# Rolling a matrix along its rows: hand-made semaphores, and the last 64 columns of 128 rows as a ladder of small DMAs

## The chip, the cores and the metric

The kernel runs on one core of one Trainium2 chip. The metric is the device time of one execution in microseconds (us), lower is better. It was timed 13 times.

## What is computed

```python
def setup_inputs():
    return {
        "x": np.random.randn(8192, 8192).astype(np.float32),
        "shift": 100,
    }

def reference(x: np.ndarray, shift: int) -> np.ndarray:
    return np.roll(x, shift, axis=1)
```

Every row of 8192 float32 (32,768 B) is rotated to the right by 100 columns: `out[r, 100:] = x[r, :8092]` and `out[r, :100] = x[r, 8092:]`. Nothing is calculated; 268.4 MB are read from the chip's main memory (HBM) and 268.4 MB are written to it.

## The kernel before

With `shift` 100 the kernel has `s = 100`, `a = 128` (s rounded up to 128) and `g = a - s = 28`. It splits every output row in two.

The **bulk** is `out[:, 128:] <- x[:, 28:8092]`, 8064 columns or 32,256 B of every row, copied from HBM to HBM with no stop in on-chip memory. The row number is taken apart as `c*64 + e*4 + j` with 16 values of `e` and 4 of `j`. One DMA (L37) takes one `j`, all 16 `e` and 32 of the 128 `c`: 512 row pieces, 16.5 MB. The `e` dimension stands first, so that each of the 16 DMA engines gets the rows of one `e`, 32 row pieces of each DMA. There are 16 such DMAs, issued in turn by two queues: SP takes `j` = 0 and 2, ACT takes `j` = 1 and 3, eight DMAs each.

The **heads** are `out[:, :128]`, 512 B of every row. They take two stages (`k` = 0, 1) of 4096 rows each, by way of on-chip tiles. POOL issues three DMAs (L67) that load, for rows with `q` = 1 to 3 of each group of four, 128 contiguous values that straddle the row boundary (the last 100 of the row before and the first 28 of the row itself), and two more (L68, L71) for the parts that remain. VectorE then puts the pieces together in a tile `h` (L69, L72), and POOL stores it with four DMAs (L76) for each stage.

The kernel has no order written out by hand: the framework that builds it adds all waits. It gives each DMA one of a fixed set of semaphores, eight for the DMAs of SP and ACT together and eight for POOL's, so that the fifth DMA of SP (and of ACT) waits until its first has landed, the sixth for the second, and so on, and POOL's second L68 and L71 wait for earlier loads. At the end SP waits for the last use of every semaphore, and a barrier of all engines ends the program (shown at L107, the line of the `with` in the launch function; L93 is the program's construction with its first barrier).

Of the kernel before, what the change touches and what calls it, by code (L numbers as in the profile page):

```python
# [1 line left out]

# [4 lines left out]


@with_exitstack
def kernel(  # L10
    ctx: ExitStack,
    tc: tile.TileContext,
    x: bass.AP,
    shift: int,
    out: bass.AP,
):
    nc = tc.nc
    n_rows, n_cols = x.shape
    s = shift % n_cols
    a = -(-s // 128) * 128  # L20
    g = a - s
    P = nc.NUM_PARTITIONS
    engines = [nc.sync, nc.scalar]
    n_chunks = 16
    rows = n_rows // n_chunks

    xm = x.rearrange("(c e j) w -> j e c w", e=16, j=4)  # L30
    om = out.rearrange("(c e j) w -> j e c w", e=16, j=4)
    depth = n_rows // 64 // 4
    for c in range(4):
        for j in range(4):
            if a < n_cols:
                cs = slice(c * depth, (c + 1) * depth)
                engines[j % 2].dma_start(out=om[j, :, cs, a:], in_=xm[j, :, cs, g:n_cols - s])  # L37
    if a == 0:
        return


    if a > 512:
        for i in range(n_chunks):
            r = slice(i * rows, (i + 1) * rows)
            nc.gpsimd.dma_start(out=out[r, :s], in_=x[r, n_cols - s:])
            if g > 0:
                nc.gpsimd.dma_start(out=out[r, s:a], in_=x[r, :g])
        return

    Q, J = 4, 8
    n_st = n_rows // (P * Q * J)
    reads = ctx.enter_context(tc.tile_pool(name="reads", bufs=n_st))
    heads = ctx.enter_context(tc.tile_pool(name="heads", bufs=n_st))
    xt = x.rearrange("(k p j q) c -> k q p j c", q=Q, j=J, p=P)
    ot = out.rearrange("(k p j q) c -> k q p j c", q=Q, j=J, p=P)
    tiles = []  # L60
    for k in range(n_st):
        t = reads.tile([P, Q - 1, J, a], x.dtype)
        h = heads.tile([P, Q, J, a], x.dtype)
        for q in range(1, Q):
            lead = bass.AP(tensor=x.tensor, offset=(k * P * J * Q + q) * n_cols - s,
                           ap=[[J * Q * n_cols, P], [Q * n_cols, J], [1, a]])
            nc.gpsimd.dma_start(out=t[:, q - 1], in_=lead)  # L67
        nc.gpsimd.dma_start(out=h[:, Q - 1, :, :s], in_=xt[k, Q - 1, :, :, n_cols - s:])  # L68
        nc.vector.tensor_copy(h[:, :Q - 1, :, :s], t[:, :, :, :s])  # L69
        if g > 0:  # L70
            nc.gpsimd.dma_start(out=h[:, 0, :, s:], in_=xt[k, 0, :, :, :g])  # L71
            nc.vector.tensor_copy(h[:, 1:, :, s:], t[:, :, :, s:])  # L72
        tiles.append(h)
    for k, h in enumerate(tiles):
        for q in range(Q):
            nc.gpsimd.dma_start(out=ot[k, q, :, :, :a], in_=h[:, q])  # L76


# [1 line left out]
_INS = ['x', 'shift']  # L80
_OUTS = [((8192, 8192), 'float32')]

_NUMBERS = {'shift': 100}


# [26 lines left out]
```

## Time and profile before

| What | Value |
|---|---|
| Time, median of 13 runs | 820.45 us (816.65 to 823.09) |
| The profiled execution's own time | 820.08 us |
| Its span, first to last instruction | 818.3 us |
| VectorE busy | 3.7 us |
| POOL busy | 16.1 us |
| DMA packets and bytes | 10784, 272.63 MB |
| Bulk DMAs | 8 on SP and 8 on ACT, 16128 KB each |
| Head DMAs on POOL | 10 loads, 8 stores |

How to read it: SP, ACT and POOL only hand out transfers; the 16 DMA engines carry them out, each taking row pieces (packets) from three queues, which the profile names q1, q10 (the two hardware queues, of SP and of ACT) and q0 (POOL's). "GB/s" counts the bytes that DMAs moved; a byte copied from HBM to HBM counts once there, but is a read and a write for the HBM. "DMA share" is the mean busy share of the 16 engines. The span leaves out what lies around it, here 820.08 - 818.3 = 1.78 us.

### The profile page before, as it was taken

How to read it: one execution, taken by the hardware profiler on the slowest of the kernel's cores; microseconds unless marked ns; L12 is line 12 of the kernel's file. 1: busy time of each engine (PE TensorE's matmuls, PEld its weight loads, DVE VectorE, ACT ScalarE, POOL GpSimd, SP SyncE). 2: the span in 40 equal slices, each digit the busy share in tenths (PEclk: the TensorE clock that was granted, in tenths of full speed). 3: DMA queues.
4: the chain of work that ended last, by engine and by line, in shares of the span. 5: the costliest groups of instructions: out<-in, count | busy, mean ns of one | idle time of the engine just before them, and what ended most of it. 6: DMA issues, size and time to landing. Idle time of an engine off the chain costs nothing. (4 is left out here: it accounts for less than half of the span.)

```text
span 818.3 us, 93 instructions
## 1 busy us (share of the span) xinstructions
DVE 3.7 (0%) x4; POOL 16.1 (2%) x22
## 2 busy tenths in 40 slices
DVE  0000000000000000000000000000000000000000
POOL 3000001000010000000000000000000000000000
DMA  9999999999999999999999999999999999999996
GB/s 309 334 333 336 335 343 329 342 334 337 347 337 344 342 347 339 342 347 337 340 340 346 341 328 330 326 333 337 328 333 330 328 328 337 326 326 334 331 331 262
DMA packets 10784, 272.63 MB, mean 333 GB/s; under 512 B 544, under 2 KB 544, under 8 KB 2592
## 3 DMA queue, kind: packets, MB, share of 16 engines
q10 hardware_dynamic: 4224, 132.12, 46.8%
q1 hardware_dynamic: 4224, 132.12, 46.8%
q0 software_dynamic: 2336, 8.39, 4.7%
HBM read 268.44 MB, written 268.44 MB: 656 GB/s over the span
## 5 line engine op out<-in xcount | busy, mean ns | idle before, releaser
L76 POOL DMA_DIRECT2D out_dram<-h x8 | 6.9, 957 | 170.8 <-DMA h<-in_x_dram 144.7
L67 POOL DMA_DIRECT2D t<-in_x_dram x6 | 5.4, 911 | 0.8 <-PEq L107 0.8
L69 DVE COPY h<-t 128x2400 f32<-128x2400 f32 x2 | 2.8, 1410 | 208.4 <-DMA t<-in_x_dram 208.4
L71 POOL DMA_DIRECT2D h<-in_x_dram x2 | 1.8, 882 | 28.7 <-DMA t<-in_x_dram 28.7
L68 POOL DMA_DIRECT2D h<-in_x_dram x2 | 1.8, 884 | 26.8 <-DMA t<-in_x_dram 26.8
L72 DVE COPY h<-t 128x672 f32<-128x672 f32 x2 | 1.0, 504 | 0.0
L93 POOL MEMSET const-float32-0.0<- 128x1 f32 x1 | 0.1, 98 | 0.2 <-issue 0.2
L93 POOL MEMSET const-bfloat16-1.0<- 128x1 bf16 x1 | 0.1, 101 | 0.0
L93 POOL MEMSET const-float32-1.0<- 128x1 f32 x1 | 0.1, 98 | 0.0
L93 POOL MEMSET const-uint8-127<- 128x1 uint8 x1 | 0.1, 98 | 0.0
## 6 DMA issues: line engine op xcount, KB each, us to landing
out_dram<-in_x_dram ACTq DMA_DIRECT2D x8, 16128.0 KB, 401.6
out_dram<-in_x_dram SPq DMA_DIRECT2D x8, 16128.0 KB, 402.4
out_dram<-h POOLq DMA_DIRECT2D x8, 512.0 KB, 183.9
t<-in_x_dram POOLq DMA_DIRECT2D x6, 512.0 KB, 118.3
h<-in_x_dram POOLq DMA_DIRECT2D x2, 400.0 KB, 151.8
h<-in_x_dram POOLq DMA_DIRECT2D x2, 112.0 KB, 146.4
```

Source lines behind the costliest of these rows:

```text
L67: nc.gpsimd.dma_start(out=t[:, q - 1], in_=lead)
L68: nc.gpsimd.dma_start(out=h[:, Q - 1, :, :s], in_=xt[k, Q - 1, :, :, n_cols - s:])
L69: nc.vector.tensor_copy(h[:, :Q - 1, :, :s], t[:, :, :, :s])
L71: nc.gpsimd.dma_start(out=h[:, 0, :, s:], in_=xt[k, 0, :, :, :g])
L72: nc.vector.tensor_copy(h[:, 1:, :, s:], t[:, :, :, s:])
L76: nc.gpsimd.dma_start(out=ot[k, q, :, :, :a], in_=h[:, q])
L93: nc = _bacc.Bacc("TRN2", target_bir_lowering=False, num_devices=1)
```

## The change

- All DMAs, waits and copies stand in one critical section (`tc.tile_critical()`), in which the framework adds no waits of its own. The kernel has its own semaphores: `bulk0` and `bulk1` for the bulk of SP and ACT, `rest`, `landed0/1` for the loads of the two head stages, `paired` for the copies of VectorE and `stored` for the stores of the heads. SP, ACT and POOL each wait at their end for all that they issued.
- The bulk is cut into `c` = 0-32, 32-64, 64-96, 96-126 and 126-128; the last cut, the rows from 8064 on, ends at column `v` = 8128 (8000 columns wide). Each queue so issues ten bulk DMAs.
- The last 64 columns of the last 128 rows are copied by 30 small DMAs. SP, after its bulk, issues 15: 8 rows of 64 columns, then 15, 14, ... 2 rows with 47, 46, ... 34 columns. ACT issues the remaining columns of these rows (15 rows of 17, 14 of 18, ... 2 of 30) and a last one with the 64 columns of the very last row. In the program's order ACT's 15 stand ahead of ACT's bulk, as they are issued in the loop's pass for SP.
- The heads keep their DMAs and copies, in the same order.

The diff, without the branch for shifts that are not used here and without setup lines:

```diff
-    engines = [nc.sync, nc.scalar]
-    n_chunks = 16
-    rows = n_rows // n_chunks
+    rings = (nc.sync, nc.scalar)
 ...
-    depth = n_rows // 64 // 4
-    for c in range(4):
-        for j in range(4):
-            if a < n_cols:
-                cs = slice(c * depth, (c + 1) * depth)
-                engines[j % 2].dma_start(out=om[j, :, cs, a:], in_=xm[j, :, cs, g:n_cols - s])
+    blocks = n_rows // 64
 ...
+    with tc.tile_critical():
+        expect = {}
+
+        def issue(eng, sem, o, i):
+            eng.dma_start(out=o, in_=i).then_inc(sem, 16)
+            expect[sem] = expect.get(sem, 0) + 16
+
+        rest = nc.alloc_semaphore("rest")
+        for q, ring in enumerate(rings):
+            bulk = nc.alloc_semaphore(f"bulk{q}")
+            if a < n_cols:
+                v = n_cols - 64
+                for c0, c1, hi in ((0, 32, n_cols), (32, 64, n_cols), (64, 96, n_cols),
+                                   (96, blocks - 2, n_cols), (blocks - 2, blocks, v)):
+                    for j in range(q, 4, 2):
+                        issue(ring, bulk, om[j, :, c0:c1, a:hi], xm[j, :, c0:c1, g:hi - s])
+                if q == 0:
+                    r = n_rows - 128
+                    for k in (8, *range(15, 1, -1)):
+                        w = 64 if k == 8 and r == n_rows - 128 else 32 + k
+                        issue(ring, bulk, out[r:r + k, v:v + w], x[r:r + k, v - s:v + w - s])
+                        if w < 64:
+                            issue(nc.scalar, rest, out[r:r + k, v + w:], x[r:r + k, v + w - s:n_cols - s])
+                        r += k
+                    issue(nc.scalar, rest, out[r:, v:], x[r:, v - s:n_cols - s])
+            if bulk in expect:
+                ring.wait_ge(bulk, expect[bulk])
+        if rest in expect:
+            nc.scalar.wait_ge(rest, expect[rest])
 ...
-        for q in range(1, Q):
-            nc.gpsimd.dma_start(out=t[:, q - 1], in_=lead)
-        nc.gpsimd.dma_start(out=h[:, Q - 1, :, :s], in_=xt[k, Q - 1, :, :, n_cols - s:])
-        nc.vector.tensor_copy(h[:, :Q - 1, :, :s], t[:, :, :, :s])
+            for q in range(1, Q):
+                issue(pooled, landed, t[:, q - 1], lead)
+            issue(pooled, landed, h[:, Q - 1, :, :s], xt[k, Q - 1, :, :, n_cols - s:])
+            if g > 0:
+                issue(pooled, landed, h[:, 0, :, s:], xt[k, 0, :, :, :g])
+            nc.vector.wait_ge(landed, expect[landed])
+            nc.vector.tensor_copy(h[:, :Q - 1, :, :s], t[:, :, :, :s]).then_inc(paired, 1)
 ...
+        for k in range(n_st):
+            pooled.wait_ge(paired, (k + 1) * per)
+            for q in range(Q):
+                issue(pooled, stored, ot[k, q, :, :, :a], heads[k][:, q])
 ...
+        if stored in expect:
+            pooled.wait_ge(stored, expect[stored])
```

More of the change, by code (lines that the diff above doesn't have):

```diff
@@ L38 @@
[L38 to L45, printed above, removed]
-            if g > 0:
[L47 to L63, printed above, removed]
-        for q in range(1, Q):
-            lead = bass.AP(tensor=x.tensor, offset=(k * P * J * Q + q) * n_cols - s,
-                           ap=[[J * Q * n_cols, P], [Q * n_cols, J], [1, a]])
-            nc.gpsimd.dma_start(out=t[:, q - 1], in_=lead)
-        nc.gpsimd.dma_start(out=h[:, Q - 1, :, :s], in_=xt[k, Q - 1, :, :, n_cols - s:])
-        nc.vector.tensor_copy(h[:, :Q - 1, :, :s], t[:, :, :, :s])
[L70 to L73, printed above, removed]
@@ L74 @@
-    for k, h in enumerate(tiles):
-        for q in range(Q):
-            nc.gpsimd.dma_start(out=ot[k, q, :, :, :a], in_=h[:, q])
+    blocks = n_rows // 64
+    Q, J = 4, 8
+    narrow = 0 < a <= 512
+    n_st = n_rows // (P * Q * J) if narrow else 0
+    pool = ctx.enter_context(tc.tile_pool(name="heads", bufs=1))
+    reads = [pool.tile([P, Q - 1, J, a], x.dtype, name=f"reads{k}") for k in range(n_st)]
+    heads = [pool.tile([P, Q, J, a], x.dtype, name=f"heads{k}") for k in range(n_st)]
+    with tc.tile_critical():
[6 more added lines that the diff above has]
+            bulk = nc.alloc_semaphore(f"bulk{q}")
+            if a < n_cols:
+                v = n_cols - 64
[16 more added lines that the diff above has]
+            nc.scalar.wait_ge(rest, expect[rest])
+        pooled = nc.gpsimd
+        paired = nc.alloc_semaphore("paired")
+        stored = nc.alloc_semaphore("stored")
+        xt = x.rearrange("(k p j q) c -> k q p j c", q=Q, j=J, p=P)
+        ot = out.rearrange("(k p j q) c -> k q p j c", q=Q, j=J, p=P)
+        n_pair = 0
+        for k in range(n_st):
+            t, h = reads[k], heads[k]
+            landed = nc.alloc_semaphore(f"landed{k}")
+            for q in range(1, Q):
+                lead = bass.AP(tensor=x.tensor, offset=(k * P * J * Q + q) * n_cols - s,
+                               ap=[[J * Q * n_cols, P], [Q * n_cols, J], [1, a]])
+                issue(pooled, landed, t[:, q - 1], lead)
+            issue(pooled, landed, h[:, Q - 1, :, :s], xt[k, Q - 1, :, :, n_cols - s:])
+            if g > 0:
+                issue(pooled, landed, h[:, 0, :, s:], xt[k, 0, :, :, :g])
+            nc.vector.wait_ge(landed, expect[landed])
+            nc.vector.tensor_copy(h[:, :Q - 1, :, :s], t[:, :, :, :s]).then_inc(paired, 1)
+            n_pair += 1
+            if g > 0:
+                nc.vector.tensor_copy(h[:, 1:, :, s:], t[:, :, :, s:]).then_inc(paired, 1)
+                n_pair += 1
+        per = n_pair // n_st if n_st else 0
+        for k in range(n_st):
+            pooled.wait_ge(paired, (k + 1) * per)
+            for q in range(Q):
+                issue(pooled, stored, ot[k, q, :, :, :a], heads[k][:, q])
+        if a > 0 and not narrow:
+            for r in range(0, n_rows, 512):
+                issue(pooled, stored, out[r:r + 512, :s], x[r:r + 512, n_cols - s:])
+                if g > 0:
+                    issue(pooled, stored, out[r:r + 512, s:a], x[r:r + 512, :g])
+        if stored in expect:
+            pooled.wait_ge(stored, expect[stored])
```

## The prediction

> **What bounds the kernel now.** I read the page's strip of 40 slices and its table of queues first, then the windows over stretches of the span, then the issues of L37, then the waits of SP's queue. The page:
>
> ```profile
> DMA  9999999999999999999999999999999999999996
> GB/s 309 334 333 336 335 343 329 342 334 337 347 337 344 342 347 339 342 347 337 340 340 346 341 328 330 326 333 337 328 333 330 328 328 337 326 326 334 331 331 262
> ...
> q10 hardware_dynamic: 4224, 132.12, 46.8%
> q1 hardware_dynamic: 4224, 132.12, 46.8%
> q0 software_dynamic: 2336, 8.39, 4.7%
> HBM read 268.44 MB, written 268.44 MB: 656 GB/s over the span
> ```
>
> The 16 DMA engines are busy from the second slice to the last but one, and the three shares add up to 98.3%. There is no stretch without a transfer, so only a higher rate or a shorter start or end can save time. Which of the two limits it, engines or memory, is seen at the end, in the windows:
>
> ```profile
> core 0: us, DVE busy (x) POOL busy (x), PEclk, DMA share, GB/s
> 0.00:5.00 5.00, 0.00 (x0) 3.91 (x9) 1.00 0.63 206
> 5.00:10.00 5.00, 0.00 (x0) 3.45 (x4) 1.00 0.97 335
> ...
> 600.00:700.00 100.00, 0.00 (x0) 0.00 (x0) 1.00 1.00 331
> ...
> 790.00:800.00 10.00, 0.00 (x0) 0.00 (x0) 1.00 0.92 329
> 800.00:805.00 5.00, 0.00 (x0) 0.00 (x0) 1.00 0.81 323
> 805.00:810.00 5.00, 0.00 (x0) 0.00 (x0) 1.00 0.75 323
> 810.00:812.00 2.00, 0.00 (x0) 0.00 (x0) 1.00 0.60 258
> 812.00:814.00 2.00, 0.00 (x0) 0.00 (x0) 1.00 0.75 323
> 814.00:816.00 2.00, 0.00 (x0) 0.00 (x0) 1.00 0.38 161
> 816.00:818.30 2.30, 0.00 (x0) 0.00 (x0) 1.00 0.00 0
> ```
>
> From 790 us on some engines have nothing left, yet 92% of them move 329 GB/s and 75% (12 of 16) still 323. The bound is thus what all engines share, the HBM at about 2 x 330 = 660 GB/s, and not the engine: 323/12 = 27 GB/s is what one engine does when fewer compete, against 331/16 = 20.7 in the middle. The packet records say the same: 32,256 B take 1.19 us at the least and 1.47 at the median. The stamps of the last bulk landings show who is early: one engine is through at 758.5 us, three at 796 to 803, twelve between 813.6 and 817.4.
>
> What is lost at the ends: from 0 to 5 us (335-206)*5/335 = 1.9 us; from 810 us on (75*2 + 10*2 + 172*2 + 333*2.3)/333 = 3.8 us, of which 0.94 lies behind the last landing at 817.36. So the ends hold under 6 us together, most of it latency.
>
> ```profile
> L37 SPq DMA_DIRECT2D out_dram<-in_x_dram x4: 607/643/97766, 0.7 to 2.8; - x4
> L37 ACTq DMA_DIRECT2D out_dram<-in_x_dram x4: 670/927/99802, 0.7 to 3.4; - x4
> ...
> SPq L37 <- DMA out_dram<-in_x_dram: 47.8, 4, 17.0
> ```
>
> These are the L37 issues that fall in the first 100 us, and SP's own waits. Three issues of each queue take 0.6 to 0.95 us, the fourth 98 us: it is held until the queue has room, so nearly three DMAs always stand ready (each lasts about 103 us). The waits for semaphores, 47.8 us in four, are spent with such a queue full.
>
> **What the Trainium skill says.** "DMA: Bandwidth & Descriptors", section "Queues, rings and completion order": an engine goes round the queues that have work, packet by packet, and all queues share the same 16 engines. The equal 46.8% agree. The same page, "Why a DMA increments its semaphore by 16 and not by 1": a DMA from SP or ACT uses as many engines (at most 16) as divide its outer dimension, from the lowest number up. So the ladder lies on engines 0 and 1 most and hardly on 14; no transfer of before shows this. The same page, "Specifications": below 512 B a transfer is a read-modify-write. All ladder rows are 256 B or less. The pieces of 400 and 112 B here go to on-chip memory, so no row of this trace prices one from HBM to HBM. "HBM Reference", "Specifications (TRN2)": 716 GB/s for the stack that two cores share; the measured 656 is 92% of it.
>
> **The change part by part.** Against the profiled execution, span 818.3.
>
> 1. *Waits between bulk DMAs go* (SP's 47.8 us and ACT's like them). Worth 0: the queues hold work for 200 to 300 us meanwhile, and even the engine that runs ahead by 59 us (758.5 against 817.4) leaves them non-empty. Were the cover gone, it would be up to 17 us for each. POOL's waits between loads (26.8 and 28.7 us) go too; its loads stay in the same order in one queue that is served packet by packet. The heads end by 466 us, 350 before the end, so 0.
> 2. *Gate at the entry.* Entering the section adds a no-op on SP for which all others wait. The barriers of before need 0.04 to 0.12 us from signal to wake-up; I take +0.15 (0.05 to 0.4) on the first transfer. It can't be negative, as the first barrier stays.
> 3. *ACT's 15 small DMAs stand ahead of its bulk.* Issues at 0.67 to 0.95 us: 15 * 0.67 = 10 us (up to 14) for which ACT's first bulk DMA is late. SP's queue alone must feed the engines meanwhile. It can: the trace's first 32 packets all come from SP's queue, and the second of each engine took 1.31 to 1.35 us, shorter than the 1.47 median. So 0 (at most 5 us, half of 10, were one queue to run at half rate, which those packets exclude). Of this remains a shift: SP gets ahead by 10/1.4 = 7 packets for each engine, and at the end ACT runs alone for about as many.
> 4. *Bulk recut.* Per queue and engine 32*8 = 256 row pieces as before, two DMAs more, so two completion writes of 9 ns. The 64 columns taken out are 128*256 B / 16 = 2 KB for each engine, 0.08 us at 27 GB/s: -0.1 together.
> 5. *SP's ladder behind its bulk.* 15 issues, but they enter the queue as soon as there is room, at some 500 to 600 us (before, the eighth issue ended at 498.7), so the issue is hidden under 200 us of bulk. What counts is the engine's time. Engines 0 and 1 get 15 pieces, and so down to 2 on engine 13 and one on 14. Lower bound of a piece: 10 ns by its bytes (256 B at 27 GB/s), as a completion write's 9 ns. Upper: POOL's loads, 4096 B read from HBM in small rows, average 0.46 us in the first 60 us, three times their 0.15 us of bytes; a read that waits on a loaded HBM may cost as much for one row. I take 0.15 us, between: 15*0.15 = 2.2 us on engines 0 and 1. It falls after SP's last bulk packet, in the last 10 us, where 12 engines each run at their own limit and nothing hides it. Which engines are early the trace doesn't tell; if engine 0 is of the twelve late ones (3 in 4), which end within 3.8 us, it moves the end by part of its load. I take +0.9 (0 to 6, from 10 ns and 0.46 us).
> 6. *ACT's ladder at the start*: the same pieces while memory is the bound and others take what an engine leaves: 0 to +0.3, I take 0.1.
> 7. *Gate at the exit.* Each queue waits itself, SP waits for all, then the old final barrier: two more hops, +0.2 (0 to 0.5).
>
> Sum: 0.15 - 0.1 + 0.9 + 0.1 + 0.2 = +1.25, span 819.5, own time 821.3. The profiled execution lies 0.37 below the median of 820.45; against the median it is 821.7. I forecast **821.7 us**, no change by a hair: 0.2% is 1.64 us, about what a measurement of this kernel can tell. The case's own range is 819.8 to 824.
>
> **The rivals.**
>
> *Slower: the ladder stalls its engines.* At 0.46 us a piece, engines 0 and 1 get 6.9 us behind their bulk, and engines 2 to 5 nearly as much, where only 3.8 us of spread lie. +5, so about 825.5. For it: rows under 512 B, and reads that wait at a loaded HBM. Against: even the 112 B rows of POOL's loads come 27 to a packet of 3024 B in 0.49 us, 18 ns each, so small rows can be piped. It decides from about 0.25 us a piece.
>
> *Faster: the two queues out of step are kinder to the HBM.* Before, ACT's row piece is the neighbour of SP's and lands 3 us later throughout; now they are 7 packets or more apart. The rate isn't a constant of nature: slices go from 326 to 347 GB/s, and once the heads are done they stay near 330. One engine that drifted out of the herd lands two DMAs (64 row pieces) in 88.2 us from 669 to 757 us, 1.38 us a piece, where the herd needed 1.58 (101 us, from 616.7 to 717.6). If the mean rises by 0.8%, 820.45 - 6.5 = 814. Against: HBM traffic is near 660 GB/s whatever the mix (with the heads, 343 GB/s counted, of which some 19 are heads and load it once: 2*343 - 19 = 667). An end in which all engines stop together would belong here too, for at most 2 us.
>
> *The change doesn't do what it says: ACT's small DMAs are stuck behind SP's blocked fourth issue.* If the two queues share what makes the descriptors, ACT's bulk would begin after 50 us or later, and SP's be done by half time. As one queue feeds the engines, the time stays about 821. Against: ACT's fourth and fifth issues ended 2.6 and 5.0 us after SP's, not in the same breath.
>
> **How the numbers follow.** Forecast 0.52 (same 0.33, slower 0.17, faster 0.02), stalling ladder 0.19 (slower), kinder HBM 0.22 (faster 0.21, same 0.01), stuck queue 0.07 (same 0.04, slower 0.02, faster 0.01). Together faster 0.24, same 0.38, slower 0.38. The range 814 to 827 takes in most of the stalling ladder (to about +6.5) and half of the faster case; some 0.2 lie outside.
>
> **What will show it.** Right: 330 GB/s in the middle as before, SP's bulk through some 10 us ahead of ACT's, ladder packets near 0.15 us, the first bulk at 2.3 us. Step 3 is wrong if the DMA share falls in the first 15 us; step 5 if the ladder's packets take 0.4 us and the engines that end last are those that carry most of it; the rate's case holds if the slices after 450 us change by over 1%. The forecast fails if the middle's rate moves either way, which no sum of instructions can give.

## The result, and the profile after

| | Before | After |
|---|---|---|
| Median time | 820.56 us (48 runs) | 825.59 us (823.26 to 830.76, 11 runs) |
| Ratio | | 1.0067, 95% interval 1.0052 to 1.0083 |
| Span of the profiled execution | 818.3 us | 824.5 us |
| First bulk packet starts | 2.18 us | 2.49 us |
| Last packet ends | 817.03 us | 823.06 us |
| Last landing | 817.36 us | 823.39 us |
| From the last landing to the end of the span | 0.94 us | 1.06 us |

The change costs 5 us. The rows for packets and landings are from the trace's packet records and landing stamps. The page of the changed kernel:

```profile
GB/s 305 337 344 335 336 335 334 337 338 338 335 343 334 339 345 341 333 338 345 331 335 328 330 326 333 326 332 338 330 329 324 326 330 335 327 329 319 336 326 245
DMA packets 11372, 272.63 MB, mean 331 GB/s; under 512 B 1132, under 2 KB 1132, under 8 KB 3180
...
q10 hardware_dynamic: 4526, 132.12, 47.7%
q1 hardware_dynamic: 4510, 132.13, 47.2%
q0 software_dynamic: 2336, 8.39, 3.7%
HBM read 268.44 MB, written 268.44 MB: 651 GB/s over the span
```

588 packets are new, all under 512 B: the ladders' row pieces and the additional completion writes. They hold no visible share of the engines' time, but the mean rate is 651 GB/s where it was 656. Where that is lost, the windows show (GB/s is the last column), first the changed kernel, then the kernel before over the same three middle stretches:

```profile
5.00:10.00 5.00, 0.00 (x0) 5.00 (x7) 1.00 0.99 336
10.00:15.00 5.00, 0.00 (x0) 0.41 (x1) 1.00 0.91 293
15.00:20.00 5.00, 0.00 (x0) 0.00 (x0) 1.00 1.03 367
...
20.00:200.00 180.00, 1.83 (x2) 3.48 (x4) 1.00 1.00 337
200.00:500.00 300.00, 1.83 (x2) 3.47 (x4) 1.00 1.00 337
500.00:780.00 280.00, 0.00 (x0) 0.00 (x0) 1.00 1.00 329
...
805.00:810.00 5.00, 0.00 (x0) 0.00 (x0) 1.00 0.86 310
...
812.00:814.00 2.00, 0.00 (x0) 0.00 (x0) 1.00 0.74 306
...
816.00:818.00 2.00, 0.00 (x0) 0.00 (x0) 1.00 0.60 257
...
820.00:822.00 2.00, 0.00 (x0) 0.00 (x0) 1.00 0.34 144
822.00:824.50 2.50, 0.00 (x0) 0.00 (x0) 1.00 0.00 0
```

```profile
20.00:200.00 180.00, 1.83 (x2) 5.23 (x6) 1.00 1.00 336
200.00:500.00 300.00, 1.83 (x2) 3.47 (x4) 1.00 1.00 341
500.00:780.00 280.00, 0.00 (x0) 0.00 (x0) 1.00 0.99 330
```

The engines are as busy as before in the middle (share 1.00), and from 200 us on they still move less. From the packet records, with the bytes of the heads counted half as they touch the HBM once, 255.30 MB are through by 780 us instead of 256.90; 1.13 MB of these 1.60 are lost between 200 and 500 us. At 330 GB/s they are 4.8 us (the later start included) of the 6.2 by which the profiled spans differ. The other 1.2 us come in the tail: from 812 us on the engines end one by one (shares 0.74, 0.60 and 0.34: twelve, ten and five of 16), where in the kernel before twelve stopped within 3.8 us. The exit adds 0.1.

The ladder itself can be followed, as its packets have a size of their own for each DMA (an extract of the packet records; one packet per engine):

```
ACT's ladder, start of the packets, us
 68 B, 15 engines    5.6 ..  5.9
 72 B, 14 engines    8.6 ..  9.6
 76 B, 13 engines   12.2 .. 14.2
 ...
116 B,  3 engines   46.2 .. 48.5
120 B,  2 engines   50.4 .. 52.3
 16 B, 16 engines   16.4 .. 55.3   (ACT's bulk follows)
each of these takes 9 to 13 ns; SP's ladder packets take 13 to 18 ns
```

A step is 3 to 4 us although a packet takes 11 ns. Between two of them each engine moves two 32,256 B pieces of SP's queue (counted in e4 below): the small packet uses one turn of the round between queues and its completion write another. So ACT's queue gets to its bulk after 16 us on the engine with no row of the ladder (the first bulk packet starts at 19.7 us), and after 55 us on the one with the whole of it. That ACT's queue did issue in time is shown by its line for the first 14 us: 17 issues, while SP's fourth was held for 82 us.

```profile
L44 ACTq DMA_DIRECT2D out_dram<-in_x_dram x17: 571/737/1560, 0.9 to 13.8; - x17
...
L44 SPq DMA_DIRECT2D out_dram<-in_x_dram x4: 598/694/82342, 1.0 to 3.1; - x4
```

### The profile page after: what moved, and what is told of

It reads as the page before. It is cut to its first block, busy times and chain, and to the rows that moved or that the text cites. A ratio compares the mean times of both kernels' runs of the same rounds, so it can differ in the third digit from the quotient of the medians.

```text
span 824.5 us, 130 instructions
## 1 busy us (share of the span) xinstructions
DVE 3.7 (0%) x4; POOL 16.1 (2%) x22
## 5 line engine op out<-in xcount | busy, mean ns | idle before, releaser
L44 POOL DMA_DIRECT2D out_dram<-heads x8 | 7.0, 1006 | 217.5 <-DVE heads L96 217.5
L44 POOL DMA_DIRECT2D reads<-in_x_dram x6 | 5.4, 910 | 1.1 <-PEq L140 1.1
L93 DVE COPY heads<-reads 128x2400 f32<-128x2400 f32 x2 | 2.8, 1410 | 227.5 <-DMA heads<-in_x_dram 227.5
L44 POOL DMA_DIRECT2D heads<-in_x_dram x4 | 3.5, 882 | 0.0
```

What stands on the lines that cost most here:

```text
L44: eng.dma_start(out=o, in_=i).then_inc(sem, 16)
L93: nc.vector.tensor_copy(h[:, :Q - 1, :, :s], t[:, :, :, :s]).then_inc(paired, 1)
```

## The experiments

All times are against the kernel before on the same chip and in the same rounds. First, four kernels that take the change apart.

**e1: the critical section alone.**

```diff
-                                   (96, blocks - 2, n_cols), (blocks - 2, blocks, v)):
+                                   (96, blocks, n_cols)):
-                if q == 0:
-                    r = n_rows - 128
...
```

> The critical section with its own semaphores, the bulk in four cuts of full width, no recut and no ladder. Theory A (ACT's ladder ahead of its bulk spends one turn of every engine's round for each small packet and each completion write, so that ACT falls behind SP, by 30 turns on engine 0 and 2 on engine 15): this is the kernel before within 1.5 us, 820.6 plus 0.3 for the gates, about 821. Theory B (the ladders cost the engines time at the end): also 821. Theory C (the section itself, with deeper queues and no waits between bulk DMAs, lowers the rate from 200 us on): about 824 to 825, with 329 GB/s between 200 and 500 us where before has 333 or more.

Measured: 821.31 against 820.17, ratio 1.0023 (1.0013 to 1.0033). The rate in the middle stays (340 GB/s from 200 to 500 us, 332 from 500 to 780), so the section and the missing waits don't lower it. But from the last landing to the end of the span it takes 2.16 us, not 0.94. The waits of SP's queue, of e1 and then of the changed kernel:

```profile
SPq L40 <- DMA out_dram<-in_x_dram: 312.6, 1, 312.6
SPq L40 <- POOLq L40: 0.9, 1, 0.9
```

```profile
SPq L40 <- DMA out_dram<-in_x_dram: 156.1, 1, 156.1
SPq L40 <- ACTq L40: 1.9, 1, 1.9
```

At the exit of the section SP waits for the others, and POOL drains, which takes 1.1 us, only once SP's own wait is over. In e1 that stands open behind the last landing. In the changed kernel SP is through at 821.33 us and ACT at 823.41, so POOL's drain is hidden behind ACT's last packets.

**e2: with the recut, no ladder.**

```diff
-                                   (96, blocks - 2, n_cols), (blocks - 2, blocks, v)):
+                                   (96, blocks - 2, n_cols), (blocks - 2, blocks, n_cols)):
-                if q == 0:
-                    r = n_rows - 128
...
```

> As the first kernel, with the last bulk cut split into 30 and 2 blocks at full width, no ladder. Theories A and B: 821, as the first kernel. Theory C: as the first kernel, 824 to 825. Only if the split at the end matters by itself does it differ from the first kernel by over 1 us.

Measured: 822.10 against 820.17, ratio 1.0026 (1.0014 to 1.0038). No different from e1: the recut costs nothing that shows.

**e3: ACT's ladder moved behind ACT's bulk.**

```diff
-                        if w < 64:
-                            issue(nc.scalar, rest, out[r:r + k, v + w:], x[r:r + k, v + w - s:n_cols - s])
                         r += k
-                    issue(nc.scalar, rest, out[r:, v:], x[r:, v - s:n_cols - s])
+                else:
+                    r = n_rows - 128
+                    for k in (8, *range(15, 1, -1)):
+                        w = 64 if k == 8 and r == n_rows - 128 else 32 + k
+                        if w < 64:
+                            issue(ring, bulk, out[r:r + k, v + w:], x[r:r + k, v + w - s:n_cols - s])
+                        r += k
+                    issue(ring, bulk, out[r:, v:], x[r:, v - s:n_cols - s])
```

> The changed kernel with ACT's 15 small DMAs moved behind ACT's bulk; all else the same. Theory A: ACT's bulk starts at 1 us as SP's does, the loss goes, about 821. Theory B: both ladders now stand unhidden at the end, so it stays at 825.6 or gets worse, up to 828, with a DMA share that falls before the last landing. Theory C: 825.

Measured: 826.43 against 820.17, ratio 1.0076 (1.0063 to 1.0090), as theory B has it. But the engines are not what is held up. The windows of e3's end:

```profile
816.00:818.00 2.00, 0.00 (x0) 0.00 (x0) 1.00 0.41 176
818.00:820.00 2.00, 0.00 (x0) 0.00 (x0) 1.00 0.23 29
820.00:822.00 2.00, 0.00 (x0) 0.00 (x0) 1.00 0.00 0
822.00:824.00 2.00, 0.00 (x0) 0.00 (x0) 1.00 0.00 0
824.00:826.40 2.40, 0.00 (x0) 0.00 (x0) 1.00 0.00 0
```

No packet runs after 819.54 us, yet the last landing is stamped 824.28. An engine puts its share of the 30 small DMAs through in half a microsecond, and their completions arrive one after the other, 4.74 us in all (0.33 of it any last packet needs). The last stamps are evenly 0.17 to 0.18 us apart: one engine, with the completions of both queues in a single series. (The next expectations take 4.74/30 = 0.16 us, close to that as this engine carries most of the 30.) With the exit that makes 6.9 us behind the last packet where before has 1.27; the 5.6 between them are nearly all of e3's loss. Its middle is sound (331 GB/s from 500 to 780 us). So e3 removes one loss and brings another of the same size.

**e4: ACT's ladder replaced by 15 DMAs that all use 16 engines.**

```diff
-                    for k in (8, *range(15, 1, -1)):
...
+                    for n in range(15):
+                        r = n_rows - 128 + n // 2 * 16
+                        w = v + n % 2 * 32
+                        issue(nc.scalar, rest, out[r:r + 16, w:w + 32], x[r:r + 16, w - s:w + 32 - s])
+                    issue(ring, bulk, out[n_rows - 16:, v + 32:], x[n_rows - 16:, v + 32 - s:n_cols - s])
```

> ACT's ladder ahead of its bulk is replaced by 15 DMAs of 16 rows by 32 columns, so that every engine spends the same 15 small packets and 15 completion writes; SP has one such DMA at its end and no ladder. Theory A in its first form (what counts is that ACT's queue lags SP's by 30 turns, on whichever engines): 825 to 827. Theory A in its second form (what counts is that the lag differs from engine to engine, which pulls the engines apart): 821. Theory B: 821, as no ladder stands at the end. Theory C: 825.

Measured: 823.91 against 820.17, ratio 1.0043 (1.0028 to 1.0058): between the two forms of theory A, and the changed kernel's interval begins inside this one's. ACT's first bulk DMA landed at about 158 us, SP's at 60. As all engines have the same ladder here, the turns can be counted: before ACT's first bulk packet, at 53.4 us, SP's queue started 30.4 pieces per engine, two for each of the 15 small DMAs.

A second set asked what in ACT's position costs, and checked the completions.

**e5: ACT on rows far from SP's, not late.**

```diff
-                for c0, c1, hi in ((0, 32, n_cols), ...):
+                cuts = [(0, 32, n_cols), (32, 64, n_cols), (64, 96, n_cols), (96, blocks, n_cols)]
+                for c0, c1, hi in cuts[2 * q:] + cuts[:2 * q]:
```

> The kernel of e1 (critical section, four full cuts, no ladder) with ACT's cuts in the order 64-96, 96-128, 0-32, 32-64: ACT copies rows 4096 away from SP's, but isn't late. Theory L (the rate falls because the two queues work on rows far apart): 2.5 to 4 us above e1's 821.3, that is 824 to 825, with the loss spread over the middle. Theory T (distance is nothing; what the changed kernel loses comes from ACT's lateness itself, in the tail that ACT drains alone with engines that end at different times): 821.3 as e1, within 1 us.

Measured: 822.36 against 820.69, ratio 1.0020 (1.0004 to 1.0037), as e1. Theory L falls: the distance between the two queues' rows costs nothing that shows.

**e6: SP's ladder alone, at the end.**

```diff
-                        w = 64 if k == 8 and r == n_rows - 128 else 32 + k
-                        issue(ring, bulk, out[r:r + k, v:v + w], x[r:r + k, v - s:v + w - s])
...
+                    for k in (8, *range(15, 0, -1)):
+                        issue(ring, bulk, out[r:r + k, v:], x[r:r + k, v - s:n_cols - s])
+                        r += k
```

> The changed kernel with no ladder on ACT; SP's 16 small DMAs at its end take the full 64 columns. Theory S (completions of small DMAs land one after the other, at about 4.74/30 = 0.16 us each, as e3 showed between its last packet and last landing): last landing some 2.4 us behind the last packet, time 2 us above e2's 822.1, about 824. If the completions are not serial, the gap is 0.33 us as in before and the time 822. Theories L and T: ACT isn't late, so nothing of the changed kernel's own loss is here.

Measured: 823.72 against 820.69, ratio 1.0038 (1.0024 to 1.0053). The last landing is 2.60 us behind the last packet (2.4 expected), the serial completions confirmed. The engine that ended last has 14 small rows behind its last bulk packet, and its last stamps are 0.18 us apart.

**e8: the same with rows of 512 B**, `v = n_cols - 128`.

> As e6 with rows of 128 columns, 512 B, in SP's ladder and the bulk's last cut 64 columns narrower. If the landing is slow because rows under 512 B are a read-modify-write: the gap between last packet and last landing shrinks to under 1 us and the time is about 822. If each completion costs whatever the row's size: 2.4 us and 824 as e6.

Measured: the gap is 1.33 us instead of 2.60; the time 824.09 against 820.69, ratio 1.0052 (1.0034 to 1.0071), doesn't show the gain. The shorter gap is not a cheaper completion. The engine that ended last has only 7 small rows behind its last bulk packet here, and its stamps follow each other as in e6 (an extract of the landing stamps, which name no engine; the series is read from its even steps):

```
last stamps of the engine that ended last, us
e6  817.26  817.44  817.62  817.80  817.98  818.16   (14 rows of 256 B and less)
e8  818.43  818.60  818.76  818.93  819.10  819.27   (7 rows of 512 B and less)
```

That is 0.18 us for a completion with 256 B and 0.17 us with 512 B. So each costs about the same whatever the row's size, as the second explanation has it, and the length of the gap depends on which engine ends last.

**e7: both ladders behind their queue's first bulk DMA.**

```diff
                         issue(ring, bulk, om[j, :, c0:c1, a:hi], xm[j, :, c0:c1, g:hi - s])
+                        if c0 == 0 and j == q:
+                            r = n_rows - 128
+                            for k in (8, *range(15, 1, -1)):
+                                w = 64 if k == 8 and r == n_rows - 128 else 32 + k
+                                lo, hi2 = (v, v + w) if q == 0 else (v + w, n_cols)
+                                if lo < hi2:
+                                    issue(ring, bulk, out[r:r + k, lo:hi2], x[r:r + k, lo - s:hi2 - s])
+                                r += k
...
```

> Both ladders of the changed kernel, each right behind its queue's first bulk DMA: neither holds ACT back at the start nor ends the program, but engines 0 and 1 still carry most of it. Theories L, T and S: nothing of the loss is left but the gates and the recut, 822 as e2, last landing 0.33 us behind the last packet. If the ladder itself costs engine time or sets the engines apart wherever it stands: 824 to 826.

Measured: 823.71 against 820.69, ratio 1.0044 (1.0027 to 1.0061). The gap behind the last packet is down to 0.51 us, but 822 was missed by 1.7 us (1.1 with e2 and e7 each taken against the kernel before). The middle of the profiled execution is slow (329 GB/s from 500 to 780 us), but that execution was the slowest of its six, 2.2 us above their median.

The last set separates ACT's lateness from the small packets that cause it.

**e9 and e10: ACT late without any small DMA.** e1, with one (e10: two) of SP's first DMAs on a semaphore `first`:

```diff
+                    if q == 1 and c0 == 0:
+                        ring.wait_ge(first, expect[first])
                     for j in range(q, 4, 2):
-                        issue(ring, bulk, ...)
+                        ahead = q == 0 and c0 == 0 and j < 2   # e10: j < 4
+                        issue(ring, first if ahead else bulk, ...)
```

> The kernel of e1 with no small DMA at all; ACT waits until SP's first bulk DMA has landed (about 50 us) and then issues its bulk. Theory T (ACT's lateness itself costs, whatever causes it): the queue that lags drains alone at the end as in e4, 823.5 to 824.5, with 329 to 330 GB/s between 500 and 780 us. Theory P (what costs is small packets and their completions standing early in a queue): as e1, 821.3 or less, since here the exit of the section waits for ACT with POOL's drain already done (1.1 us less than e1).

> As e9, but ACT waits for two SP DMAs (about 100 us). Theory T: the loss of e9 grows, 825 to 827. Theory P: as e1, 820 to 821.3.

Measured: e9 822.64 against 821.00, ratio 1.0027 (1.0017 to 1.0036); e10 821.18, ratio 1.0002 (0.9993 to 1.0012). ACT's first bulk DMA landed at about 167 and 219 us here, later than in e4 (158) and in the changed kernel (120 to 162, depending on the engine), and the loss is smaller, in e10 none. Theory T, by which e10 should lose more than e9, falls. In both POOL's drain is hidden at the exit, as expected (1.05 us). Theory P expected no loss at all, and e9's 1.6 us stay unexplained.

**e12: the changed kernel without SP's ladder.**

```diff
-                        issue(ring, bulk, out[r:r + k, v:v + w], x[r:r + k, v - s:v + w - s])
...
+                    for k in (8, *range(15, 0, -1)):
+                        issue(nc.scalar, rest, out[r:r + k, v:], x[r:r + k, v - s:n_cols - s])
+                        r += k
```

> The changed kernel without SP's ladder: ACT's 16 small DMAs, ahead of its bulk, take the full 64 columns. Both theories T and P: the loss of the changed kernel is all here, 825 to 826. If SP's ladder, which runs beside ACT's last packets, is part of it: 823 to 824.

Measured: 826.34 against 821.00, ratio 1.0070 (1.0051 to 1.0089). The whole loss is there without SP's ladder, as far as the intervals tell. The middle, of e12 and then of e10:

```profile
20.00:200.00 180.00, 1.83 (x2) 3.49 (x4) 1.00 1.00 338
200.00:500.00 300.00, 1.83 (x2) 3.48 (x4) 1.00 1.00 335
500.00:780.00 280.00, 0.00 (x0) 0.00 (x0) 1.00 1.00 328
```

```profile
20.00:200.00 180.00, 3.66 (x4) 6.97 (x8) 1.00 1.00 342
200.00:500.00 300.00, 0.00 (x0) 0.00 (x0) 1.00 1.00 338
500.00:780.00 280.00, 0.00 (x0) 0.00 (x0) 1.00 1.00 331
```

All shares are 1.00, and from 200 us on e12 moves about 1% less. (Before 200 us e10 has twice as much of the heads, whose bytes touch the HBM once where those of a copy touch it twice; with them halved both kernels move 328 to 329 GB/s there.)

**e11: another map of rows to engines**, in the kernel before:

```diff
-    xm = x.rearrange("(c e j) w -> j e c w", e=16, j=4)
-    om = out.rearrange("(c e j) w -> j e c w", e=16, j=4)
+    xm = x.rearrange("(e c j) w -> j e c w", e=16, j=4)
+    om = out.rearrange("(e c j) w -> j e c w", e=16, j=4)
```

> The kernel before with the row number taken apart as e*512 + c*4 + j, so that each DMA engine copies a block of 512 neighbouring rows and the 16 engines stand 16 MB apart instead of 128 KB. It asks whether the 330 GB/s is a fixed limit of the memory or depends on which rows are worked on at once. If fixed: 820.5. If it depends on them: away from it by over 8 us, either way.

Measured: 2040.84 us against 821.00 as the median of six, two of which were longer than the rest (2102 and 2109 us); without these two the ratio is 2.4754 (2.4651 to 2.4856). The engines are as busy as ever and the HBM gives 264 GB/s instead of 656. This is e11's page:

```profile
DMA  9999999999999999999999999999999999999998
...
HBM read 268.44 MB, written 268.44 MB: 264 GB/s over the span
```

Two things change at once, the distance between the engines (128 KB to 16 MB) and the step of one engine from piece to piece (2 MB to 128 KB). Which of them counts was not tried.

Put side by side (MB, gap and exit from one profiled execution each, from the packet records and landing stamps; "run against median" is how far that execution's own time lies from the median of its kernel; "against before" is the difference of the medians; "left" is what remains of it when the longer gap and exit are taken off):

| Kernel | Small packets early in a queue | MB through at 780 us | Run against median | Last packet to last landing | Last landing to end | Against before | Left |
|---|---|---|---|---|---|---|---|
| before | no | 256.90 | -0.5 us | 0.33 us | 0.94 us | | |
| changed | ACT | 255.30 | +0.6 | 0.33 | 1.06 | +5.0 | 4.9 |
| e12 | ACT | 254.81 | +1.0 | 0.35 | 1.06 | +5.3 | 5.2 |
| e4 | ACT, even | 255.63 | +0.6 | 0.33 | 1.05 | +3.7 | 3.6 |
| e7 | both queues | 255.78 | +2.2 | 0.51 | 2.00 | +3.0 | 1.8 |
| e1 | no | 257.22 | -0.4 | 0.34 | 2.16 | +1.1 | -0.1 |
| e2 | no | 256.01 | +1.9 | 0.34 | 2.17 | +1.9 | 0.7 |
| e3 | no | 256.44 | +1.8 | 4.74 | 2.16 | +6.3 | 0.6 |
| e5 | no | 256.69 | 0.0 | 0.33 | 2.17 | +1.7 | 0.4 |
| e6 | no | 257.32 | -1.6 | 2.60 | 2.17 | +3.0 | -0.5 |
| e8 | no | 256.59 | -0.9 | 1.33 | 2.17 | +3.4 | 1.2 |
| e9 | no | 257.06 | -3.3 | 0.35 | 1.05 | +1.6 | 1.5 |
| e10 | no | 257.01 | -0.9 | 0.35 | 1.05 | +0.2 | 0.1 |

The column of MB seems to part the four kernels with small DMAs early from the nine without, but the profiled executions are not typical ones. At 0.33 MB a microsecond, e7's, 2.2 us slower than its median, has some 0.7 MB less than a typical one, and e9's, 3.3 us faster and the fastest of 22, some 1.1 MB more; by this estimate e7 would have 256.5 MB and e9 256.0. The last column doesn't rest on this: with small DMAs ahead of ACT's bulk 3.6 to 5.2 us are left, in the eight kernels without early ones -0.5 to 1.5, each uncertain by 0.8 to 1.6 us. e7, with 1.8, can't be told from these eight.

## Why the prediction was right or wrong

The range of 814 to 827 us held the time, by luck: it was that wide for a stalling ladder and for a kinder HBM, and neither came. The forecast of 821.7 was 3.9 us too low, and the time lies outside the range of 819.8 to 824 that it gave itself. The rival "the ladder stalls its engines" named nearly the measured number, 825.5, but its mechanism is not what happened: agreement in the number is no evidence for it.

- **Bound** (HBM near 660 GB/s, engines always busy): right that no engine time was the limit. Wrong in treating the rate as nearly fixed. e11 shows that it depends on which rows the engines work on, 264 GB/s against 656.
- **Step 1**, waits that go: right at 0. e1's middle has before's rate.
- **Step 2**, entry: +0.15 was foreseen; e1's first bulk packet starts at 2.37 us against 2.18.
- **Step 3**, ACT's ladder ahead of its bulk, is the step that failed. It counted the 10 us of issue time, found SP's queue able to feed the engines meanwhile (right: 336 GB/s from 5 to 10 us, though one of the 16 packets read for it took 1.22 us and not 1.31 or more; the share falls to 0.91 from 10 to 15 us, the sign named against this step, but e2 and e3, where ACT isn't late, have 0.93 there), and left "a shift" of 7 packets at no cost. It had quoted that queues are served in turn, and did not apply it to the ladder: a packet of 11 ns uses a turn as a packet of 1.5 us does, and so does the completion write. The shift became 30 pieces of SP on the engine with all of the ladder, and 39 us between the first engine to reach ACT's bulk and the last. The ladder in this place carries the loss: it is whole in e12, with this ladder alone, and gone in e1, e2 and e6, without it, and in e3, which moves it (-0.5 to 0.7 us left in the table). e10 shows that ACT's lateness alone doesn't cost this.
- **Step 4**, the recut: right, e2 equals e1.
- **Step 5**, SP's ladder, +0.9: no cost is seen in the changed kernel (e12 without it is no faster, with an interval of 1.6 us to either side), where it runs beside ACT's late bulk. Its packets take 13 to 18 ns on the engine, close to the lower bound of 10 ns. What small rows do cost lies where the step didn't look, in the arrival of their completions: 0.17 to 0.18 us each on an engine, visible when nothing follows (e3, e6, e8). That this is near the 0.15 us which the step took for a piece is luck, as that stood between a bound by bytes and a mean of POOL's loads. (That mean counts their completion writes in; the 4096 B packets alone average 0.49 us.)
- **Step 6**, +0.1 for ACT's ladder because the memory is the bound: the same failure as step 3. The loss is not in the first microseconds; in the profiled execution most of it falls between 200 and 500 us.
- **Step 7**, exit, +0.2: 0.12 in the changed kernel, but only since ACT ends 2 us behind SP. Standing open the section's exit costs 1.2 us more than before's.
- **Rivals.** "Kinder to the HBM" went the other way: the rate did move, down, from 341 to 337 GB/s between 200 and 500 us, and after 500 us by less than the 1% that the rival named. "Stuck behind SP's issue" didn't happen: ACT issued 17 DMAs in 14 us.

Open: *why* ACT's ladder lowers the rate, for hundreds of microseconds after its last packet. Its parts were tried apart, and of none was it shown that it carries the loss: lateness without small packets leaves 1.5 and 0.1 us (e9, e10), an uneven ladder that delays neither queue against the other 1.8 (e7), lateness with an even ladder 3.6 (e4), against 4.9 and 5.2 for the changed kernel and e12. The intervals of e4 and e7 overlap with those of e2 and e9 as well as with the changed kernel's. The changed kernel sets the engines apart, 34 us between the first and the last landing of SP's first bulk DMA (before: 3.1), and e11 shows that the HBM cares which rows meet. That this is the link was only argued; no run showed it, and e4 speaks against its being all, as its engines land that DMA within 3.7 us.

No kernel tried beats the one before; e10 equals it.

## What to carry to other kernels

When several queues share the DMA engines, count turns and not bytes: every small DMA ahead of a queue's bulk hands the other queue two of its large packets, on exactly the engines the small one uses. Small DMAs at the very end cost their completions in series on each engine instead, so both ends of a program are bad places for them. And when all engines are busy, first ask which addresses they work on, since that decided far more here (e11) than any order of issue.

## What the runs showed of the hardware

- Sixteen engines that stand 16 MB apart and step by 128 KB, instead of 128 KB apart with steps of 2 MB, copy the same rows at 264 GB/s of HBM traffic instead of 656, with the same packet sizes (e11: a 32,256 B packet takes 3.8 us instead of 1.5).
- The landings of small copies from HBM to HBM on one engine are 0.17 to 0.18 us apart, with rows of 68 to 256 B (e3, e6) as with rows of 512 B (e8), though a packet is through its engine in 9 to 27 ns.
- A small packet and its completion write each take a turn of an engine's round between queues, as a packet of 1.5 us does: 15 small DMAs let the other queue start 30 large pieces first (e4).
- One engine runs ahead of the others by 59 us in the kernel before and by 84 us in e2, whose time is no different from that of e1 with 67.
